# Two blocks of tokens held in two banks: 512-wide units for values, gates and queries of a four-layer network, and the sinks as a column of the scores

## The chip, the core and the metric

The program runs on one core of one Trainium2 chip. Its time is the device time of one execution in microseconds. The core has a matrix engine (PE, with its weight loads counted apart as PEld), three engines for vectors (DVE, ACT and POOL) and a queue (SP) that starts the loads of weights from HBM. All arithmetic that matters here is fp32: each product of matrices is made of three matrix multiplications of a high and a low part (high·high, high·low, low·high).

## The reference, cut to what matters

Four layers work on 512 tokens of width 1024. Layers 0 and 1 are attention layers with a gated FFN, layers 2 and 3 have an MLP with a squared ReLU. The change touches layers 1, 2 and 3:

```python
# layer 1 (NSA): q, the first 768 columns of the projection, and the 256 of the memory's queries
# layer 2 (gated linear attention), 4 heads of 256 value features each
q, k, v, g, glr = jnp.split(h @ w_in, [GLA_DK, 2 * GLA_DK, 2 * GLA_DK + GLA_DV, 2 * GLA_DK + 2 * GLA_DV], axis=-1)
log_a = jax.nn.log_sigmoid(glr @ w_gate_up + b_gate_up) / GLA_GATE_NORMALIZER
...
o = rms_norm(o, g_norm).reshape(B, T, GLA_DV)
o = o * jax.nn.silu(g.astype(jnp.float32))
return o.astype(h.dtype) @ w_out
# layer 3 (sliding window with sinks), per head
mx = jnp.maximum(jnp.max(s, axis=-1, keepdims=True), sink)
e = jnp.exp(s - mx)
p = e / (jnp.sum(e, axis=-1, keepdims=True) + jnp.exp(sink - mx))
```

## The kernel before

Tokens stand in four blocks of 128. A **weight unit** (`wunit`, L181) is 128x1024 numbers, 512 KB: SP loads it into `raw` (3 buffers), ACT copies it to the high part `whi` (L188), and DVE (in 2 pieces of 512) or POOL (in 4 of 256) makes the low part `wlo` (L175). `whi` and `wlo` have a few buffers each, so that a unit can be made ready while another is used. Matmuls stand on lines L198 to L200 (`mm3`, one line for each of the three products).

Where the result is wanted with tokens on the partitions, `tm_steps` takes a matrix of 1024x256 as two units, holds both, and goes through the four blocks one after the other. A block is 24 matmuls of 256 columns into a PSUM bank of its own, and then its evacuation. In layer 1, `q_steps` does this for the four groups 0, 3, 1, 2 of the queries with the tag "any", which takes banks from the tags `ps` and `tr` in turn (2 banks each, 4 together). In layer 2, `v_steps(h)` (values of head h) and `g_steps(h)` (its gates) do it with the tag `gm`, which has 2 banks. Those two banks also take the 512-wide query and key matrices of the next head (`unit`, called `gla_qk` unit below).

The evacuation of a block in layer 2: values are scaled on ACT (L1424) and their low part is made on DVE (L1425). Gates go through Silu on ACT (L1475), and POOL multiplies the norm's gain in (L1476). Silu, Exp, Ln and the square root (L243) use different function tables on ACT; a change of table is an instruction of its own, ACT_TABLE_LOAD.

Layer 2 is written as lists of steps that `weave` (L97) mixes: the log gates (`gate`: matmul, Abs L1459, Exp L1460; `gate_log`: Ln L1466) with `v_steps(1)`, then for each head h the steps of its linear attention (`gla_steps`: transposes, at, ke, qs, products into `more` and `acc`, Squares L1609) with a fill: for h = 0 the next head's query and key units, `g_steps(0)` and `g_steps(1)`, for h = 1 the units, `v_steps(2)` and `g_steps(2)`, for h = 2 the units and `v_steps(3)`, for h = 3 `g_steps(3)`. A scheduler then orders the instructions of each engine; each engine works its list strictly in order.

In layer 3 a task (`swa_task`) is a block of queries for two heads: scores on PE, mask and maximum on DVE (L1724), two Exp with a sum on ACT (L1726), then the sink: POOL adds the maximum to it (L1728), ACT takes its Exp (L1729), POOL adds that to the sum (L1732), and DVE takes the reciprocal (L1734); DVE and POOL normalize one head each (L436, L445), PE transposes.

Of the kernel before, what the change touches and what calls it, by code (L numbers as in the profile page):

```python
# [10 lines left out]
F32 = mybir.dt.float32  # L11
# [98 lines left out]
class Core:  # L110
# [33 lines left out]
    def t4(self, shape=(P, S), dt=F32):  # L144
        return self.sm(shape, "sm_s", 6, dt)
# [188 lines left out]
    def tm_steps(self, act, src, width, evac, tags=("gm",) * 4, eng=None, b0=0):  # L334

        box = {}

        def load():
            box["w"] = self.tm_weights(src, width, eng)

        def block(b):
            o = self.psum(tags[b])
            for k in range(KC):
                t = slice(b * P, (b + 1) * P)
                self.mm3(o[:, :width], self.part(act[k], t), box["w"][k], k == 0, k == KC - 1)
            evac(b, o)

        return [load] + [lambda b=b: block(b) for b in range(b0, NB)]

# [835 lines left out]
    def layer1(self):  # L1185
# [35 lines left out]
        def q_steps(g):  # L1221
            def first():
                tqs[g] = self.blk([P, NB, 256], F32, "tq")

            evac = lambda b, ps: self.evac_to(tqs[g], 256, rstd)(b, ps)
            return [first] + self.tm_steps(act, self.a["w_nsa"][g], 256, evac, ("any",) * 4)
# [11 lines left out]
        def prep(g):  # L1238
# [10 lines left out]
            if g == 3:  # L1249
# [7 lines left out]
        main = (kv_steps(0) + kv_steps(1) + [gates] + q_steps(0) + q_steps(3) + self.mem_steps(1, mkv) + q_steps(1)  # L1257
                + q_steps(2))
# [136 lines left out]
    def layer2(self):  # L1395
# [35 lines left out]
        def v_steps(h):  # L1431
            return self.tm_steps(act, self.a["w_gla"][h], 256, v_evac(h), eng=self.G)

# [37 lines left out]
        def g_steps(h):  # L1471
# [6 lines left out]
            return self.tm_steps(act, self.a["w_gla"][4 + h], 256, evac, eng=self.G)  # L1478

        gates = [functools.partial(f, b) for f in (gate, gate_log) for b in range(NB)]  # L1480
        weave(gates, (v_steps(1), 0, 1))
# [11 lines left out]
        for h in range(4):  # L1493
            fill, nxt = [], {}
            if h < 3:
                fill = [lambda h=h: nxt.update(self.gla_decay(h + 1, la, rb))]
                ps = []

                def unit(i, h=h):
                    o = self.gm()  # L1500
                    self.gemm_fm(act, [self.wunit(self.a["w_glaqk"][h + 1 + i], eng=self.G)], [o])
                    ps.append(o)

                fill += [lambda: unit(0), lambda: unit(4), lambda: self.gla_qk(nxt, *ps)]
                fill += g_steps(0) + g_steps(1) if h == 0 else (finals if h == 1 else []) + v_steps(h + 1) + (g_steps(2) if h == 1 else [])
            else:
                fill = g_steps(3)
# [119 lines left out]
    def layer3(self):  # L1627
# [48 lines left out]
        for u in range(2):  # L1676
            t, f = self.t2(), self.t2()
            self.V.tensor_tensor(t, outs[u], rb, ALU.mult)
            self.V.tensor_scalar(f, t, bias(u), None, ALU.add)
            if u == 0:  # L1680
                for g in range(2):
                    r, ro = slice(g * 64, g * 64 + 64), slice(64 - g * 64, 128 - g * 64)
                    self.A.activation(kh[g][r, 0], f[r], AF.Copy)
                    self.A.activation(kh[g][ro, 0], f[r], AF.Copy)
                    self.lo(kh[g][r, 1], f[r], kh[g][r, 0])
                    self.V.tensor_copy(kh[g][ro, 1], kh[g][r, 1].bitcast(F32))
            else:
                pt = self.gm()
# [16 lines left out]
    def swa_task(self, j, b, qT, kh, vv, bufs, ns):  # L1705
# [10 lines left out]
        def softmax():  # L1716
# [3 lines left out]
            w["p"] = p = self.t4()  # L1720
            for e in range(2):
                h = 2 * j + e
                o = slice(e * 256, e * 256 + n)
                self.V.tensor_tensor_reduce(p[:, o], sc[:, o], self.swa[:, 256 - n:256], -SCALE, ns[:, h:h + 1],  # L1724
                                            ALU.add, ALU.min, accum_out=m[:, e:e + 1])
                self.A.activation(p[:, o], p[:, o], AF.Exp, bias=m[:, e:e + 1], scale=-1.0, accum_out=z[:, e:e + 1])  # L1726
            w["sk"] = sk = self.lt([P, 2], "sk", 4)
            self.G.tensor_tensor(sk, self.sinks[:, 2 * j:2 * j + 2], m, ALU.add)  # L1728
            self.A.activation(sk, sk, AF.Exp)  # L1729

        def norm():
            self.G.tensor_tensor(w["z"], w["z"], w["sk"], ALU.add)  # L1732
            r = self.sm([P, 2], "nm_r", 6)
            self.V.reciprocal(r, w["z"])  # L1734
            for e in range(2):
                self.normalize(w["p"][:, e * 256:e * 256 + n], r[:, e:e + 1], None, "VG"[e])

        def trans():
            w["tr"] = tr = self.psum("tr")
            for e in range(2):  # L1740
                for c in range(n // P):
                    s = slice(e * 256 + c * P, e * 256 + (c + 1) * P)
                    self.T.transpose(tr[:, s], w["p"][:, s], self.ident)
# [75 lines left out]
def pack(i):  # L1819
# [32 lines left out]
    o["w_nsa"] = _tm(np.concatenate([nsa[:, 0:768], nsa[:, 1572:1828]], 1), 256)  # L1852
# [11 lines left out]
    o["w_gla"] = _tm(gla[:, 1024:3072], 256)  # L1864
# [29 lines left out]
```

## Time and profile before

| | us |
|---|---|
| median of 3 runs | 2370.29 (2369.07 to 2371.36) |
| the profiled execution's own time | 2370.64 |
| its span in the profile | 2368.9 |
| PE busy | 2321.1 |
| DVE busy | 1436.7 |
| ACT busy | 1131.7 |
| POOL busy | 482.0 |

The span is what the profile's views are measured in, from the first instruction to the last; the own time holds what lies around it, 1.7 us. PE is busy for 98% of the span, so most things that the other engines do lie beside it. Layer 1's projections stand at about 592 to 720 us, layer 2's gates, values and linear attention at 1284 to 1445, layer 3's attention at 1892 to 1980.

### The profile page before, as it was taken

The page shows a single profiled execution, that of the slowest core. Times are in us where ns is not written, and L with a number is a line of the kernel's source. Part 1 is how long each engine was busy: PE and PEld are TensorE (multiplying, and loading weights), DVE is VectorE, ACT ScalarE, POOL GpSimd, SP SyncE. Part 2 cuts the span into 40 slices and gives each one's busy share as a digit, 9 for nine tenths or more (in the row PEclk, how much of TensorE's full clock was granted, in tenths as well). Part 3 has the DMA queues.
Part 4 walks back from the last instruction along what each step waited for, and adds up shares of the span by engine and source line. Part 5 has one row for each costly group of instructions (what it writes and reads, how often), then busy time and mean ns, then how long its engine had stood idle before and what let it go on. Part 6 is the DMA issues. An engine that isn't in the chain of part 4 may idle for free.

```text
span 2368.9 us, 35404 instructions
## 1 busy us (share of the span) xinstructions
PE 2321.1 (98%) x13390; PEld 2004.4 (85%) x13390; DVE 1436.7 (61%) x2980; ACT 1131.7 (48%) x2152; POOL 482.0 (20%) x738
## 2 busy tenths in 40 slices
PE   8899999999999999999999999999999999999998
PEld 8888988888997879888888998988888878988886
DVE  5996655455667676554555446744446787644446
ACT  7677522222458675222226566633225686533233
POOL 2756000000137730000001660000000171000000
PEclk9999999999999999999999999999999999999999
DMA  5213422322330114223222224432224414423224
GB/s 179 72 37 101 149 100 90 99 97 98 101 132 21 63 46 142 99 90 101 95 94 77 81 68 155 160 101 97 96 98 160 143 55 130 163 86 104 97 100 142
DMA packets 68301, 243.88 MB, mean 103 GB/s; under 512 B 7570, under 2 KB 7826, under 8 KB 68131
## 3 DMA queue, kind: packets, MB, share of 16 engines
q1 hardware_dynamic: 68130, 241.62, 30.9%
q8 instruction: 106, 1.74, 0.3%
q14 instruction: 65, 0.52, 0.1%
HBM read 239.50 MB, written 2.10 MB: 102 GB/s over the span
## 4 chain that ended last, share of the span: by engine, by line
PE 89%; DVE 7%; ACT 3%; issue 1%; DMA 1%; POOL 0%; SPq 0%; DVEq 0%; ACTq 0%; POOLq 0%
PE ps L199 11%; PE ps L200 11%; PE ps L198 11%; PE tr L198 11%; PE tr L199 11%; PE tr L200 10%; PE gm L199 3%; PE gm L198 3%; PE gm L200 3%; PE acc L529 2%; PE more L198 2%; PE more L199 2%; PE more L200 2%; PE tr L451 2%; PE ps L424 1%; PE ps L425 1%
## 5 line engine op out<-in xcount | busy, mean ns | idle before, releaser
L188 ACT ACTIVATE whi<-raw 128x1024 fp32r<-128x1024 f32 (+1 forms) x443 | 466.2, 1054 | 857.2 <-PE ps L199 223.3
L175 DVE TENSOR_TENSOR wlo<-raw,whi 128x512 fp32r<-128x512 f32 x744 | 525.7, 749 | 318.4 <-ACT whi L188 316.9
L175 POOL TENSOR_TENSOR wlo<-raw,whi 128x256 fp32r<-128x256 f32 x284 | 220.0, 805 | 628.6 <-ACT whi L188 540.6
L199 PE MATMUL ps<-act,whi 128*128 128x512 f32 (+1 forms) x712 | 257.3, 362 | 0.1
L198 PE MATMUL ps<-act,whi 128*128 128x512 f32 (+1 forms) x712 | 257.3, 362 | 0.1
L200 PE MATMUL ps<-act,wlo 128*128 128x512 f32 (+1 forms) x712 | 257.1, 361 | 0.1
L200 PE MATMUL tr<-act,wlo 128*128 128x512 f32 (+1 forms) x640 | 231.6, 362 | 0.0
L198 PE MATMUL tr<-act,whi 128*128 128x512 f32 (+1 forms) x640 | 231.5, 362 | 0.0
L199 PE MATMUL tr<-act,whi 128*128 128x512 f32 (+1 forms) x640 | 231.3, 361 | 0.0
L731 POOL TENSOR_TENSOR sm_s<-sm_s,sm_s 128x512 f32<-128x512 f32 x40 | 51.7, 1292 | 531.9 <-DVE sm_s L730 531.9
L198 PEld LDWEIGHTS ps<-act,whi 128*128 128x128 f32 x712 | 134.3, 189 | 20.7 <-ACT whi L188 0.3
L199 PEld LDWEIGHTS ps<-act,whi 128*128 128x128 f32 x712 | 134.3, 189 | 20.7 <-DVE act L302 0.3
L200 PEld LDWEIGHTS ps<-act,wlo 128*128 128x128 f32 x712 | 134.3, 189 | 20.5 <-DVE wlo L175 0.2
L199 PEld LDWEIGHTS tr<-act,whi 128*128 128x128 f32 x640 | 120.8, 189 | 18.4
L200 PEld LDWEIGHTS tr<-act,wlo 128*128 128x128 f32 x640 | 120.9, 189 | 18.4
L198 PEld LDWEIGHTS tr<-act,whi 128*128 128x128 f32 x640 | 120.8, 189 | 18.3
L445 POOL TENSOR_TENSOR sm_s<-sm_s,nm_r 128x256 f32<-128x256 f32 (+2 forms) x172 | 105.1, 627 | 45.7 <-DVE nm_r L479 23.5
L178 ACT ACTIVATE hid<-sm_s 128x512 fp32r<-128x512 f32 x88 | 55.6, 632 | 109.7 <-DVE sm_s L884 58.1
L198 PE MATMUL gm<-whi,act 128*128 128x256 f32 (+1 forms) x360 | 102.9, 288 | 1.3 <-ACT rb L280 0.6
L200 PE MATMUL gm<-whi,act 128*128 128x256 f32 (+1 forms) x360 | 102.2, 286 | 0.0
L199 PE MATMUL gm<-wlo,act 128*128 128x256 f32 (+1 forms) x360 | 101.8, 285 | 0.0
L199 PE MATMUL ps<-wlo,hid 128*128 128x512 f32 x256 | 99.8, 390 | 0.0
(665 smaller groups left out, 5810.0 us busy)
## 6 DMA issues: line engine op xcount, KB each, us to landing
raw<-in_w_down SPq DMA_DIRECT2D x124, 512.0 KB, 3.3
raw<-in_w_ffn SPq DMA_DIRECT2D x96, 512.0 KB, 3.3
raw<-in_w_up SPq DMA_DIRECT2D x80, 512.0 KB, 3.4
raw<-in_w_o SPq DMA_DIRECT2D x32, 512.0 KB, 3.3
raw<-in_w_glao SPq DMA_DIRECT2D x16, 512.0 KB, 3.4
raw<-in_w_swa SPq DMA_DIRECT2D x16, 512.0 KB, 3.4
raw<-in_w_swao SPq DMA_DIRECT2D x16, 512.0 KB, 3.3
raw<-in_w_dsa SPq DMA_DIRECT2D x14, 512.0 KB, 3.7
```

Source lines behind the costliest of these rows:

```text
L175: (eng or self.V).tensor_tensor(out, src, hi.bitcast(F32), ALU.subtract)
L178: self.A.activation(hi, src, AF.Copy)
L188: self.A.activation(hi[:, :n], raw[:, :n], AF.Copy)
L198: mm(out, l[0], r[0], start=start, stop=False)
L199: mm(out, l[0], r[1], start=False, stop=False)
L200: mm(out, l[1], r[0], start=False, stop=stop)
L424: self.T.matmul(out, q[:, t], k[0][:, k0:k0 + n], start=True, stop=False)
L425: self.T.matmul(out, q[:, t], k[1][:, k0:k0 + n], start=False, stop=True)
L445: self.G.tensor_tensor(p, p, r.to_broadcast([P, p.shape[-1]]), ALU.mult)
L451: self.T.transpose(ps[:, s], p[:, s], self.ident)
L529: return self.T.matmul(acc[e * 64:e * 64 + 64, t0:t0 + p[e].shape[-1]], v[e], p[e], start=start and i == 0, stop=stop and i == n - 1)
L731: self.G.tensor_tensor(u, u, t, ALU.mult)
```

## The change

A new function `tm_wide` takes a matrix of 1024x512 as four units; a unit is two of the eight chunks of 128 input features, 512 columns wide. It holds two blocks' results at once in two banks. Pass 0 goes through the units 0, 1, 2, 3 for blocks 0 and 1 and then evacuates both, pass 1 goes backwards through 3, 2, 1 for blocks 2 and 3 and ends with unit 0, which is loaded and split a second time. So a matrix takes five units where two matrices of 256 took four. Layer 1's queries become two such matrices. In layer 2 the values of head i+1 and the gates of head i become one for i = 0, 1, 2 (`vg_steps`), with the low part on DVE where it was on POOL; the last head's gates stay 256 wide. The fills change with it: the gates of layer 2 are woven with `vg_steps(0)`, h = 0 with the units and `vg_steps(1)`, h = 1 with the units and `vg_steps(2)`, h = 2 with the units alone, h = 3 with the last gates. In layer 3 the sink becomes a column of the scores' tile, which POOL copies in ahead; the Exp takes one column more and its sum holds the sink.

```diff
+    def tm_wide(self, act, src, evac, tag="gm", eng=None):
+        units, box = {}, {}
+        def step(p, i):
+            if i not in units:
+                units[i] = self.wunit(src[:, i * 1024:(i + 1) * 1024], eng=eng)
+            a, z = ((0, 3), (3, 0))[p]
+            if i == a:
+                box["ps"] = [self.psum(tag) for _ in range(2)]
+            self.tok_unit(units[i], act[2 * i:2 * i + 2], box["ps"], (2 * p, 2 * p + 1), i == a, i == z)
+            if i == z:
+                for b, o in zip((2 * p, 2 * p + 1), box["ps"]):
+                    evac(b, o)
+            if i == 0:
+                units.pop(0)
+        return [functools.partial(step, 0, i) for i in range(4)] + [functools.partial(step, 1, i) for i in (3, 2, 1, 0)]
...
-        main = (kv_steps(0) + kv_steps(1) + [gates] + q_steps(0) + q_steps(3) + self.mem_steps(1, mkv) + q_steps(1)
-                + q_steps(2))
+        main = (kv_steps(0) + kv_steps(1) + [gates] + q_steps(0, (0, 3)) + self.mem_steps(1, mkv)
+                + q_steps(1, (1, 2)))
...
+        def vg_steps(i):
+            box = {}
+            def first():
+                box["e"] = v_evac(i + 1), g_evac(i)
+            def evac(b, ps):
+                for n, e in enumerate(box["e"]):
+                    e(b, ps[:, n * 256:n * 256 + 256])
+            return [first] + self.tm_wide(act, self.a["w_glvg"][i], evac)
...
-        weave(gates, (v_steps(1), 0, 1))
+        weave(gates, (vg_steps(0), 0, 1))
...
-                fill += g_steps(0) + g_steps(1) if h == 0 else (finals if h == 1 else []) + v_steps(h + 1) + (g_steps(2) if h == 1 else [])
+                fill += (finals if h == 1 else []) + (vg_steps(h + 1) if h < 2 else [])
...
-            w["p"] = p = self.t4()
+            w["p"] = p = self.t4(S + 2).rearrange("p (e k) -> p e k", e=2)
+            self.G.tensor_copy(p[:, :, n], ns[:, 2 * j:2 * j + 2])
...
-                self.A.activation(p[:, o], p[:, o], AF.Exp, bias=m[:, e:e + 1], scale=-1.0, accum_out=z[:, e:e + 1])
-            w["sk"] = sk = self.lt([P, 2], "sk", 4)
-            self.G.tensor_tensor(sk, self.sinks[:, 2 * j:2 * j + 2], m, ALU.add)
-            self.A.activation(sk, sk, AF.Exp)
+                self.A.activation(p[:, e, :n + 1], p[:, e, :n + 1], AF.Exp, bias=m[:, e:e + 1], scale=-1.0,
+                                  accum_out=z[:, e:e + 1])
...
-            self.G.tensor_tensor(w["z"], w["z"], w["sk"], ALU.add)
```

In layer 3 the bias of the keys and values is also added by ACT as it copies, where DVE added it before.

The order of the instructions, first in the kernel before. On PE, at the end of the gates of head 1, the third block's bank (gm_13494) ends and the fourth block (gm_13521) begins:

```order
L200 MATMUL gm_13494<-whi_13406,act_12624 128x256
L198 MATMUL gm_13494<-whi_13406,act_12625 128x256
L199 MATMUL gm_13494<-wlo_13407,act_12625 128x256
L200 MATMUL gm_13494<-whi_13406,act_12625 128x256
L198 MATMUL gm_13521<-whi_13397,act_12618 128x256 [waits Activation_49]
L199 MATMUL gm_13521<-wlo_13398,act_12618 128x256
L200 MATMUL gm_13521<-whi_13397,act_12618 128x256
```

And on ACT, the evacuations of the four banks of the same gates (sg), with what stands between them:

```order
L1475 ACTIVATE sg_13118<-gm_13432,r_2428_12726 128x256 [waits PE_49]
L1475 ACTIVATE sg_13118<-gm_13459,r_2428_12726 128x256 [waits PE_49]
L1609 ACTIVATE t_2538_13492,oss_13122<-acc_13414 128x256 [waits PE_49]
L243 ACT_TABLE_LOAD
L243 ACTIVATE rs_s_13557<-mv_13555 128x4 [waits DVE_49]
L1475 ACT_TABLE_LOAD
L1475 ACTIVATE sg_13118<-gm_13494,r_2428_12726 128x256 [waits PE_49]
L188 ACTIVATE whi_13651<-raw_13650 128x1024 [waits DMAHW5_49,PE_49,Pool_49]
L1475 ACTIVATE sg_13118<-gm_13521,r_2428_12726 128x256 [waits PE_49]
```

Here 24 matmuls of a block stand between the end of a bank and the next use of that bank, as gm has two.

The first place in the changed kernel, on PE: the end of the first wide matrix of layer 2 (banks gm_12868 and gm_12869, values of head 1 and gates of head 0, blocks 2 and 3), and behind it the first query unit of the next head (gm_13001):

```order
L198 MATMUL gm_12869<-whi_12911,act_12433 128x512
L199 MATMUL gm_12868<-wlo_12912,act_12433 128x512 [waits DVE_49]
L200 MATMUL gm_12868<-whi_12911,act_12433 128x512
L199 MATMUL gm_12869<-wlo_12912,act_12433 128x512
L200 MATMUL gm_12869<-whi_12911,act_12433 128x512
L1602 MATMUL tr_12961<-qd_12946,sm_s_12945 128x64 [waits DVE_49]
L198 MATMUL gm_13001<-act_12432,whi_13003 128x512 [waits Activation_49]
```

And on ACT, where these two banks are evacuated (values L1448, gates L1496):

```order
L188 ACTIVATE whi_13037<-raw_13036 128x1024 [waits DMAHW4_49,PE_49]
L1448 ACTIVATE v_12761<-gm_12868,r_2426_12540 128x256 [waits PE_49]
L1448 ACTIVATE v_12761<-gm_12869,r_2426_12540 128x256 [waits PE_49]
L188 ACTIVATE whi_13095<-raw_13094 128x1024 [waits DMAHW5_49,DVE_49,Activation_49]
L1496 ACT_TABLE_LOAD
L1496 ACTIVATE sg_12762<-gm_12868,r_2426_12540 128x256 [waits DVE_49]
L1496 ACTIVATE sg_12762<-gm_12869,r_2426_12540 128x256 [waits DVE_49]
```

The query unit takes the bank of gm_12868, and three matmuls stand between that bank's last matmul and it; the gates' evacuation, which frees the bank, stands behind two evacuations of values, a copy of a weight unit and a change of table.

The second place, the end of the second wide matrix (gm_13215 and gm_13216), on PE, with the query unit of head 2 (gm_13338) behind it; L1602 and L1603 are small products of the linear attention:

```order
L200 MATMUL gm_13215<-whi_13262,act_12433 128x512
L198 MATMUL gm_13216<-whi_13262,act_12433 128x512
L199 MATMUL gm_13216<-wlo_13263,act_12433 128x512
L200 MATMUL gm_13216<-whi_13262,act_12433 128x512
L1602 MATMUL ps_13372<-qd_12984,sm_s_12983 128x64
L1603 MATMUL ps_13372<-qd_12984,sm_s_12982 128x64
L1602 MATMUL ps_13372<-qd_12984,sm_s_12983 128x64
L1603 MATMUL ps_13372<-qd_12984,sm_s_12982 128x64
L1602 MATMUL ps_13372<-qd_12984,sm_s_12983 128x64
L1603 MATMUL ps_13372<-qd_12984,sm_s_12982 128x64
L198 MATMUL gm_13338<-act_12432,whi_13340 128x512 [waits Activation_49]
```

And on ACT there (cat is the copy of head 0's gated output out of PSUM):

```order
L1448 ACTIVATE v_13077<-gm_13215,r_2426_12540 128x256 [waits PE_49]
L178 ACTIVATE cat_13302<-tr_13304 128x512
L178 ACTIVATE cat_13303<-ps_13305 128x512
L1448 ACTIVATE v_13077<-gm_13216,r_2426_12540 128x256 [waits PE_49]
L188 ACTIVATE whi_13497<-raw_13496 128x1024 [waits DMAHW4_49,DVE_49,Activation_49]
L1496 ACT_TABLE_LOAD
L1496 ACTIVATE sg_13078<-gm_13215,r_2426_12540 128x256 [waits DVE_49]
L1605 ACTIVATE t_2572_13381<-ps_13372 128x512 [waits PE_49]
```

Nine matmuls stand on PE between the last one of gm_13215 and the reuse of its bank; six instructions of ACT stand between the moment at which that bank is full and the end of its evacuation, and the evacuation itself makes seven.

The third place, the change from pass 0 to pass 1 of the second wide matrix, on ACT (t is a Square of the linear attention's output, fd a copy of its state):

```order
L1448 ACTIVATE v_13076<-gm_13101,r_2426_12540 128x256 [waits PE_49]
L1646 ACTIVATE t_2531_13149,oss_12960<-more_13079 128x256 [waits PE_49]
L1448 ACTIVATE v_13076<-gm_13102,r_2426_12540 128x256 [waits PE_49]
L1646 ACTIVATE t_2542_13213,oss_12960<-acc_13197 128x256 [waits DVE_49,PE_49]
L178 ACTIVATE fd_13210<-t_2540_13208 128x256 [waits DVE_49]
L1496 ACTIVATE sg_13078<-gm_13101,r_2426_12540 128x256 [waits DVE_49]
L1496 ACTIVATE sg_13078<-gm_13102,r_2426_12540 128x256 [waits DVE_49]
```

On PE two 512-wide and nine 256-wide matmuls stand between the last one of gm_13101 and the first of pass 1, which takes the same bank.

## Rows read from the trace of the kernel before

**Rows 1.** The page: busy time by engine, and the chain that ended last by engine.

```profile
PE 2321.1 (98%) x13390; PEld 2004.4 (85%) x13390; DVE 1436.7 (61%) x2980; ACT 1131.7 (48%) x2152; POOL 482.0 (20%) x738
...
PE 89%; DVE 7%; ACT 3%; issue 1%; DMA 1%; POOL 0%; SPq 0%; DVEq 0%; ACTq 0%; POOLq 0%
```

**Rows 2.** Windows, layer 1's projections, layer 2, layer 3's attention: stretch, length, busy times, clock.

```profile
592.00:720.00 128.00, 127.02 (x967) 121.85 (x967) 76.20 (x144) 65.23 (x126) 33.68 (x45) 1.00 0.33 109
1284.00:1445.00 161.00, 159.63 (x1132) 148.46 (x1132) 78.72 (x152) 96.24 (x168) 84.51 (x107) 0.99 0.23 76
1892.00:1980.00 88.00, 84.09 (x539) 66.99 (x538) 73.92 (x252) 71.93 (x228) 54.05 (x128) 1.00 0.24 78
```

**Rows 3.** Waits of PE, 1284 to 1445: total us, times, longest us.

```profile
PE gm L198 <- ACT rb L280: 0.6, 1, 0.6
```

**Rows 4.** Timeline of PE in layer 2: start, duration, instruction, count.

```profile
1301.80 0.28 PE L198 MATMUL gm<-whi,act 128*128 128x256 f32 x1
1301.92 0.28 PE L199 MATMUL gm<-wlo,act 128*128 128x256 f32 x1
...
1302.16 1.50 PE L1529 MATMUL ps<-consts,la 128*128 128x128 f32 x12
...
1304.43 0.39 PE L199 MATMUL gm<-act,whi 128*128 128x512 f32 x1
...
1306.95 0.39 PE L198 MATMUL gm<-act,whi 128*128 128x512 f32 x1
```

**Rows 5.** Groups of ACT, 1284 to 1445: busy, mean ns, idle before.

```profile
L188 ACT ACTIVATE whi<-raw 128x1024 fp32r<-128x1024 f32 x24 | 25.3, 1056 | 18.9 <-PE gm L199 7.2 <-issue 6.1 <-PE gm L200 3.4
L1475 ACT ACTIVATE sg<-gm,r 128x256 f32<-128x256 f32 x16 | 7.5, 474 | 10.4 <-PE gm L200 10.3
L1475 ACT ACT_TABLE_LOAD x5 | 6.4, 1283 | 0.1
...
L1424 ACT ACTIVATE v<-gm,r 128x256 fp32r<-128x256 f32 x12 | 5.6, 467 | 5.3 <-PE gm L200 5.3
...
L178 ACT ACTIVATE fd<-t 128x256 fp32r<-128x256 f32 x12 | 4.9, 417 | 2.3 <-DVE t L1602 1.5 <-DVE t L1604 0.7
...
L1609 ACT ACTIVATE t<-acc 128x256 f32<-128x256 f32 x8 | 3.0, 379 | 2.6 <-PE acc L200 2.5
...
L178 ACT ACTIVATE cat<-tr 128x512 fp32r<-128x512 f32 x3 | 1.8, 589 | 0.0
...
L1609 ACT ACTIVATION_READ_ACCUMULATOR t<-acc 128x1 f32 x8 | 1.6, 196 | 0.0
...
L1568 ACT ACTIVATE t<-ps 128x512 f32<-128x512 f32 x2 | 1.2, 603 | 0.8 <-PE ps L1566 0.8
```

**Rows 6.** Timeline of ACT at the log gates of layer 2.

```profile
1294.66 0.60 ACT L1459 ACTIVATE ge<-tr 128x512 f32<-128x512 f32 x1
1295.29 0.63 ACT L1460 ACTIVATE ge<-ge 128x512 f32<-128x512 f32 x1
1295.94 1.28 ACT L1466 ACT_TABLE_LOAD   x1
1297.24 0.72 ACT L1466 ACTIVATE ge<-ge,ones 128x512 f32<-128x512 f32 x1
```

**Rows 7.** Windows ahead of a fall of the clock and behind it, and around a gap without one.

```profile
72.00:76.80 4.80, 1.90 (x17) 1.72 (x17) 4.63 (x10) 3.44 (x13) 3.90 (x5) 1.00 0.52 168
76.80:80.40 3.60, 3.60 (x20) 3.60 (x20) 3.42 (x12) 1.28 (x4) 0.47 (x1) 0.53 0.01 3
...
148.50:158.90 10.40, 9.94 (x54) 8.29 (x51) 9.08 (x41) 8.14 (x32) 3.84 (x8) 0.51 0.07 29
...
835.50:838.50 3.00, 0.96 (x5) 0.54 (x5) 1.24 (x7) 2.80 (x6) 0.40 (x3) 1.00 0.00 0
838.50:842.00 3.50, 3.25 (x21) 1.96 (x22) 3.12 (x10) 2.67 (x8) 0.82 (x1) 1.00 0.00 0
```

**Rows 8.** Groups of layer 3's sinks, 1892 to 1980.

```profile
L1729 ACT ACTIVATE sk<-sk 128x2 f32<-128x2 f32 x32 | 5.6, 192 | 0.6 <-POOL sk L1728 0.6
```

More of the change, by code (lines that the diff above doesn't have):

```diff
@@ L142, in t2, with t4 @@
         return self.sm(shape, "t2", 3, dt)
-    def t4(self, shape=(P, S), dt=F32):
-        return self.sm(shape, "sm_s", 6, dt)
+    def t4(self, n=S):
+        return self.sm([P, S + 2], "sm_s", 6)[:, :n]
     def fd(self, shape=(P, S), dt=F32):
@@ L1219, in layer1, with q_steps @@
         tqs, qT, cTs = [None] * 4, [None] * KC, [None] * 3
-        def q_steps(g):
+        def q_steps(i, gs):
             def first():
-                tqs[g] = self.blk([P, NB, 256], F32, "tq")
-            evac = lambda b, ps: self.evac_to(tqs[g], 256, rstd)(b, ps)
-            return [first] + self.tm_steps(act, self.a["w_nsa"][g], 256, evac, ("any",) * 4)
+                for g in gs:
+                    tqs[g] = self.blk([P, NB, 256], F32, "tq")
+            def evac(b, ps):
+                for n, g in enumerate(gs):
+                    self.evac_to(tqs[g], 256, rstd, n * 256)(b, ps)
+            return [first] + self.tm_wide(act, self.a["w_nsa"][i], evac, "any")
         kT, vT = [], []
@@ L1469, in layer2, with g_evac @@
         sgs = {}
-        def g_steps(h):
+        def g_evac(h):
             sgs[h] = sg = self.blk([P, NB, 256], F32, "sg")
@@ L1504, in layer2 @@
                 fill += [lambda: unit(0), lambda: unit(4), lambda: self.gla_qk(nxt, *ps)]
-                fill += g_steps(0) + g_steps(1) if h == 0 else (finals if h == 1 else []) + v_steps(h + 1) + (g_steps(2) if h == 1 else [])
+                fill += (finals if h == 1 else []) + (vg_steps(h + 1) if h < 2 else [])
             else:
-                fill = g_steps(3)
+                fill = g_steps()
             weave(prev + self.gla_steps(cur, vp.pop(h)), (fill, 0, 1))
@@ L1676, in layer3 @@
         for u in range(2):
-            t, f = self.t2(), self.t2()
+            t = self.t2()
             self.V.tensor_tensor(t, outs[u], rb, ALU.mult)
-            self.V.tensor_scalar(f, t, bias(u), None, ALU.add)
             if u == 0:
@@ L1682, in layer3 @@
                     r, ro = slice(g * 64, g * 64 + 64), slice(64 - g * 64, 128 - g * 64)
[L1683 to L1686, printed above, removed]
-            else:
+                    bs = bias(u)[r]
+                    for i in (r, ro):
+                        self.A.activation(kh[g][i, 0], t[r], AF.Identity, bias=bs)
+                        self.V.scalar_tensor_tensor(kh[g][i, 1], t[r], bs, kh[g][r, 0].bitcast(F32), ALU.add, ALU.subtract)
+            else:
+                f = self.t2()
+                self.A.activation(f, t, AF.Identity, bias=bias(u))
                 pt = self.gm()
@@ L1735, in norm @@
             for e in range(2):
-                self.normalize(w["p"][:, e * 256:e * 256 + n], r[:, e:e + 1], None, "VG"[e])
+                self.normalize(w["p"][:, e, :n], r[:, e:e + 1], None, "VG"[e])
         def trans():
@@ L1742, in trans @@
                     s = slice(e * 256 + c * P, e * 256 + (c + 1) * P)
[L1743 removed]
+                    self.T.transpose(tr[:, s], w["p"][:, e, c * P:(c + 1) * P], self.ident)
         def s2():
@@ L1863, in pack @@
     o["w_down"] = np.stack([_down(f("ffn_w_down")[l]) for l in range(2)])
-    o["w_gla"] = _tm(gla[:, 1024:3072], 256)
+    gv, gg = gla[:, 1024:2048], gla[:, 2048:3072]
+    o["w_glvg"] = np.stack([_tm(np.concatenate([gv[:, h * 256 + 256:h * 256 + 512], gg[:, h * 256:h * 256 + 256]], 1), 512)[0]
+                            for h in range(3)])
+    o["w_glg"] = _tm(gg[:, 768:1024], 256)[0]
     o["w_glv"] = _tm(np.concatenate([gla[:, 1024:1280], gla[:, 3072:3088]], 1), 272)[0]
```

14 lines of the change are left out of this document (7 added, 7 removed).

## The prediction

> **What bounds the kernel now.** I read the page first. PE is busy for 2321.1 of 2368.9 us and holds 89% of the chain that ended last [rows 1], so a step on another engine counts only where PE has to wait for it. The windows of the three stretches that are touched say how near PE is to its limit in each [rows 2]: in layer 1's projections it idles 1.0 us of 128, in layer 2 1.4 of 161, in layer 3's attention 3.9 of 88. The longest wait of PE in layer 2 is 0.6 us, and it stands before the gates [rows 3]: the evacuations there, which end in ACT's Silu, are all hidden at present. That hiding is what I look at below, since ACT has only 96.24 of the 161 us filled and would look idle enough from the page.
>
> **What the wide matmuls save.** The durations mislead: 0.28 us for 256 columns and 0.39 for 512, but neighbours overlap. The starts tell the cost [rows 4]: 0.12 us from one 256-wide matmul to the next, and (1306.95 - 1304.43)/11 = 0.229 us for the 512-wide, 11 of which start in that time. Two narrow ones cost 0.240, one wide 0.229: 0.011 us saved. A matrix of 1024x512 has 3 x 8 x 4 = 96 wide matmuls, so a pair of old matrices saves 1.06 us. Layer 1 has two such pairs, -2.1 us, layer 2 three, -3.2 us. Together -5.3, which needs a PE without waits.
>
> **What the reload costs.** Each pair loads and splits a fifth unit: one more `whi` copy of 1.056 us on ACT [rows 5]. Five of them stand beside PE, since ACT has over 60 us free in each of the stretches of layers 1 and 2 [rows 2]. Unit 0's second copy takes the buffer of unit 3, the first one that pass 1 is done with, and has two units, 24 matmuls or 5.5 us, before it is wanted. I take nothing. If its cover were gone, PE would wait for copy and low part once in each pair; the copy alone is 5.3 us in all.
>
> **Banks in layer 1.** The tag "any" has four banks; the second pass takes the other two, so an evacuation has 48 matmuls or 11 us of cover. Nothing.
>
> **Banks in layer 2.** Here `gm` has two, both are full at the same time at the end of a pass, and the next user of `gm` waits until the first of them is empty. That bank is emptied by two ACT evacuations (values 0.467, gates 0.474 us) with DVE's part between, and ACT takes them in its own order, with other work and a change of table (1.283 us) in between [rows 5]. Before, one block lay between the end of a bank and its next use, 24 x 0.12 = 2.9 us. Each place is PE's work up to the reuse of the bank against ACT's up to the end of its evacuation; small matmuls count 1.50/12 = 0.125 us [rows 4].
> - End of matrix 1 (first place of the order): ACT has values twice, a weight copy, a table, the gates: 0.934 + 1.056 + 1.283 + 0.474 = 3.75 us. PE has two wide ones and a small one, 0.58. Stall 3.2.
> - End of matrix 2 (second place): values twice 0.934, `cat` twice 1.178, weight copy 1.056, table 1.283, gates 0.474: 4.93. PE: three wide, six small, 1.44. Stall 3.5.
> - End of matrix 3: as the last, with one copy of 0.603 more (t from ps), 5.53. PE: three wide and ten small, 1.94. Stall 3.6.
> - Pass change in matrix 2 (third place): two values 0.934, two Squares with their reads 2 x 0.575, fd 0.417, gates 0.474: 2.97. PE: 2 x 0.229 + 9 x 0.12 = 1.54. Stall 1.4.
> - Pass change in matrix 3: only the second Square's result is late: behind the first Square's matmuls stand 1.2 us of PE against 0.575 + 0.575 + 0.474 on ACT. Stall 0.4.
> - Pass change in matrix 1, among the log gates: from the last gate's matmul ACT has Abs, Exp and a table, 1297.24 - 1294.66 = 2.58, four Ln of 0.72 [rows 6], values 0.467, a table, gates 0.474: 7.7. PE has 23 wide and 8 small, 6.3. Stall 1.4.
> - The last head: its gates lost the fill around them; behind `qs` stand a table and Silu, 1.76, against 8 narrow matmuls, 0.96. Stall 0.8.
>
> Sum 14.3 us. In each of these waits everything of PE stands still, the linear attention's products among it; ACT, DVE and POOL get no later than PE. So the stall is not made up: PE was full before. If the gates' evacuations came ahead of the table and the weight copy, the sum would fall to near 0; if DVE's part of the values is late too (its row before is hidden), it grows. I keep 5 to 18 as ends.
>
> **Does a change of table cost more than its row?** The row of the load says 1.28 us, and its neighbours stand close: Exp ends at 1295.92, the load goes from 1295.94 to 1297.22, Ln begins at 1297.24 [rows 6]. So 1.28 is the whole price here and the sum goes by that. The Trainium skill, "ScalarE: Activation LUTs", section "What ACT_TABLE_LOAD costs", gives about 1283 ns for the load and about 1380 ns of drain with it, some 2.66 us for every switch. The trace agrees on the load and shows no drain. What a dearer switch would do is the third rival.
>
> **The clock.** After 2.9 us without work in the 4.8 us to 76.8, PE's granted clock fell to about half (0.53) for 3.6 us; another fall lasted 10.4 us (0.51). A gap of 2.0 us in a stretch of 3.0 was followed by no fall [rows 7]. A fall of 3.6 us loses 3.6 x 0.47 = 1.7 us of work, one of 10.4 loses 5.1. Three of the stalls above (3.2, 3.5, 3.6) are longer than 2.9. I count falls of the short kind behind two of them, +3.4; the ends are 0 and 3 x 5.1 = 15.
>
> **Layer 3.** ACT loses 32 small Exp, 32 x 0.192 = 6.1 us, of a stretch in which it is busy 71.93 of 88 and DVE 73.92 [rows 2, 8]. POOL loses two small additions a task and gains one copy, which stands in POOL's list behind its normalizations, and DVE's mask waits for it. The copy has no row; it is bounded by nothing (hidden, as POOL has 34 us free) and by the 6.1 us that ACT gives back. PE idles 3.9 us there: between 0 and 6.1 I take half of the idle time, -2. The bias on ACT instead of DVE is a few instructions ahead of the attention: nothing.
>
> **Sum.** -5.3 + 14.3 - 2 + 3.4 = +10.4. Own time 2370.64 + 10.4 = 2381.0; the median of the runs is 0.35 below the profiled execution, so 2380.7 us. A change under 0.2% (4.7 us) can't be told from none here.
>
> **The rivals.**
> - Faster: the Silu of a pass's first bank runs as soon as the bank is full, so PE waits no more than before. Then -5.3 and layer 3's -2 to -6 stay: 2361 (2359 to 2363). For it: ACT idles 65 us of layer 2's 161. Against: ACT's list is worked in order, and it has a table and a weight copy ahead of the gates at the end of each of the three matrices. It decides if the stalls of all seven places together are below some 2.6 us. Chance 0.14.
> - No change: half of the hand sum, 7.2, against -5.3 and -2, no fall of the clock: 2370 (2366 to 2375). For it: I let ACT begin each chain only when the bank is full, and have PE's rows at their shortest. Chance 0.2.
> - Slower by more: a switch of table holds ACT for another 1.28 us at five of the places (the three ends, the first pass change, the last head): +6.4, 2387. That is the drain that the page names. The rows above speak against it. Or each of the three long stalls brings a fall of the clock of the long kind, up to 2392. Chance of both 0.1.
> - My forecast, 2380.7 (2375 to 2386): chance 0.56.
>
> **How the numbers follow.** The range goes from the upper part of the faster case, 2364, to the long falls, 2390; that leaves out most of the faster case (0.11) and the tail above (0.06). Of the forecast's own 0.56 all lies above the bound of 2375.0; with the dearer cases slower has 0.66, no change 0.2, faster 0.14.
>
> **What would show it.** Right: in layer 2, PE waits for ACT's gates (sg) at the bank of the first matmul of the three query units or output products behind each wide matrix, 3 us and more each, and 14 us in all; layer 1's projections shorter by about 2 us; no ACT Exp of the sinks and an attention of 86 us. Wrong: no PE wait over 1 us between 1284 and 1445, which would bring the faster case; or a wait of DVE for POOL's copy in layer 3 that pulls PE with it, which would add to the time where I take some off.

## The result

| | us |
|---|---|
| before, median of 4 runs | 2369.76 (2369.07 to 2371.36) |
| changed, median of 4 runs | 2392.1 (2390.11 to 2393.1) |
| ratio | 1.0083, interval 1.0071 to 1.0096 |

By the medians the change makes the kernel slower by 22.3 us, by the ratio by 0.83%, 19.7 us; the interval holds both. That is the way that was forecast, but about twice the size (+10.4). The median lies 2 us above the upper end of the range, 2390, and 2369.76 times the ratio, 2389.4, just below it. In the profiled executions the span went from 2368.9 to 2390.6 us.

### Where it went, by stage

Two instructions that stand in both kernels mark the stages: the transposes at the start of layer 2's log gates (L1446 before, L1467 after) and those of layer 3's values (L1690, L1728). First the kernel before, by source line (count, duration ns as least/median/most, first and last start):

```profile
L1446 PE MATMUL tr<-consts,gl x4: 272/272/273, 1283.5 to 1283.8; 128*16 128x128 f32 x4
...
L1690 PE MATMUL gm<-consts,t x4: 270/272/272, 1885.3 to 1885.6; 128*128 128x128 f32 x4
```

The same in the changed kernel:

```profile
L1467 PE MATMUL tr<-consts,gl x4: 272/272/273, 1289.1 to 1289.5; 128*16 128x128 f32 x4
...
L1728 PE MATMUL gm<-consts,t x4: 270/272/272, 1908.6 to 1908.9; 128*128 128x128 f32 x4
```

Up to the log gates the changed kernel is 5.6 us late, up to layer 3's values 23.3, at the end 21.7. So layers 0 and 1 lost 5.6, layer 2 with its MLP 17.7, and layer 3 with its MLP gave 1.6 back. Layer 0 is the same code in both, and 0.6 of the 5.6 lie ahead of layer 1: its first 274-wide matmul starts at 617.56 before and at 618.15 after. That leaves 5.0 for layer 1. My terms for layers 1, 2 and 3 were -2.1, +14.5 (-3.2 + 14.3 + 3.4) and -2.

### The profile after

The page, busy time by engine; PE has 4.7 us more of it than in [rows 1] with fewer instructions, as matmuls at half clock count for longer:

```profile
PE 2325.8 (97%) x12910; PEld 1986.0 (83%) x12910; DVE 1449.4 (61%) x3012; ACT 1135.2 (47%) x2127; POOL 440.6 (18%) x658
```

The waits of PE in the changed kernel's layer 2, 1284 to 1470 (total us, times, longest):

```profile
PE gm L198 <- ACT sg L1496: 10.1, 4, 4.3
PE tr L1659 <- DVE sg L1657: 2.1, 1, 2.1
PE tr L1618 <- DVE t L1614: 0.9, 1, 0.9
PE acc L198 <- ACT t L1646: 0.7, 1, 0.7
PE gm L198 <- ACT rb L280: 0.6, 1, 0.6
PE more L198 <- ACT at L178: 0.5, 1, 0.5
```

The first row is the predicted wait: a matmul into `gm` waits for the gates' Silu that still reads the bank. All rows together are 14.9 us; before, the same stretch had 1.3, the longest 0.6 [rows 3]. The four waits of the first row are 0.64 at the pass change of matrix 1, and 3.56, 4.30 and 1.56 at the ends of the three matrices. The timeline of PE at the end of the first wide matrix (start, duration, and at a row's end the idle time and what ended it):

```profile
1318.91 0.39 PE L199 MATMUL gm<-wlo,act 128*128 128x512 f32 x1
1319.14 0.39 PE L200 MATMUL gm<-whi,act 128*128 128x512 f32 x1
1319.37 0.33 PE L1602 MATMUL tr<-qd,sm_s 128*128 128x64 f32 x2
1323.26 0.50 PE L198 MATMUL gm<-act,whi 128*128 128x512 f32 x1 [3.56 <-ACT sg L1496]
```

and of ACT at the same time:

```profile
1319.11 0.93 ACT L1448 ACTIVATE v<-gm,r 128x256 fp32r<-128x256 f32 x2 [1.21 <-PE gm L200]
1320.36 1.06 ACT L188 ACTIVATE whi<-raw 128x1024 fp32r<-128x1024 f32 x1 [0.32 <-DMA raw<-in_w_glvg]
1321.43 1.28 ACT L1496 ACT_TABLE_LOAD   x1
1322.73 0.84 ACT L1496 ACTIVATE sg<-gm,r 128x256 f32<-128x256 f32 x2
```

Values, weight copy, change of table, gates: the chain is link by link the one of the prediction's first place. The stall is 3.56 us where 3.2 were worked out; 0.32 of it is a wait of the weight copy for its load, which I had not counted. The load of the table takes 1.28 us, and 0.02 after it Silu starts, so the drain of the Trainium skill, "ScalarE: Activation LUTs", section "What ACT_TABLE_LOAD costs", does not show here either, and the rival that rests on it falls.

Layer 1 is where I expected nothing but a gain. The waits of PE there, 680 to 760 us:

```profile
PE ps L444 <- ACT sm_s L652: 7.2, 3, 5.6
PE gm L198 <- DVE t L598: 1.7, 1, 1.7
PE gm L1387 <- DVE cs L1382: 0.5, 1, 0.5
PE acc L549 <- DVE qT L175: 0.4, 1, 0.4
PE tr L471 <- DVE pt L539: 0.2, 1, 0.2
```

Before, the same stretch held 5.5 us of waits, none over 1.3. The 5.6 us stand at the scores of the memory's attention, and the view names ACT's Exp. But ACT itself was idle then; the timeline of DVE tells who was late (L648 and L649 make the maximum that the Exp needs, L435 to L438 are the rope of the queries):

```profile
720.56 0.69 DVE L648 TENSOR_REDUCE mm_m<-ps 128x2 f32<-128x512 f32 x1 [4.23 <-PE ps L445]
721.28 0.24 DVE L649 TENSOR_SCALAR mm_m<-mm_m 128x2 f32<-128x2 f32 x1
721.44 1.03 DVE L435 TENSOR_TENSOR t<-tq,consts 128x256 f32<-128x256 f32 x1
722.39 1.37 DVE L436 TENSOR_TENSOR t<-tq,consts 128x128 f32<-128x128 f32 x1
...
726.00 0.80 DVE L437 TENSOR_TENSOR t<-tq,consts 128x128 f32<-128x128 f32 x1
726.73 0.41 DVE L438 TENSOR_TENSOR tq<-t,t 128x256 f32<-128x256 f32 x1
727.06 0.68 DVE L648 TENSOR_REDUCE mm_m<-ps 128x2 f32<-128x512 f32 x1
```

Seven instructions of the rope of two groups stand between the first maximum and the second (the cut leaves out three of them). Before, the queries of groups 1 and 2 were ready one after the other, and only the last instruction of one rope (L418) stands between the first two maxima.

The third loss is the clock. Windows over the stretches in layers 1 and 2 in which the granted clock had fallen (the column behind POOL's):

```profile
1325.00:1328.20 3.20, 3.20 (x9) 2.43 (x9) 0.00 (x0) 0.00 (x0) 0.03 (x1) 0.50 0.63 241
1372.60:1376.00 3.40, 3.39 (x8) 2.71 (x9) 1.52 (x2) 2.05 (x4) 3.37 (x4) 0.50 0.54 153
1440.90:1451.00 10.10, 9.51 (x42) 8.68 (x43) 5.34 (x11) 5.46 (x10) 1.34 (x2) 0.50 0.01 2
686.50:689.90 3.40, 3.27 (x15) 3.27 (x16) 3.31 (x7) 2.72 (x5) 2.56 (x4) 0.50 0.38 139
727.50:734.20 6.70, 4.34 (x20) 4.05 (x21) 5.72 (x19) 4.07 (x16) 5.02 (x9) 0.50 0.25 78
```

In layer 2 these are 16.7 us at half clock, 8.4 us of work lost if PE had work all the time; before there was one fall of 3.4 us, 1.7 lost, and it came with no wait of PE over 0.6 us in the 8 us ahead of it. The first of the three begins 1.5 us after the end of the wait of 3.56 us, the second right at the end of the wait of 4.30, the long one in PE's wait of 2.1 us for DVE's gating. In layer 1 there are 10.1 us against 3.4 before. Layer 2's MLP ends with a fall in both kernels, this one before and one of 3.4 us at 1901.6 after:

```profile
1875.70:1882.60 6.90, 6.15 (x15) 4.83 (x16) 5.04 (x9) 2.90 (x5) 3.34 (x5) 0.51 0.50 169
```

With that the stages can be added up. Layer 1: -2.1 for the pitch, +4.5 of waits (10.0 against 5.5), +3.4 of clock: 5.8, and 5.0 were found. Layer 2 with its MLP: -3.2 for the pitch, +13.6 of waits (14.9 against 1.3), +5.0 of clock (+6.7 for the three falls, -1.7 for the shorter one at the end): 15.4, and 17.7 were found. The difference lies where the pitch's saving should be. If the length of this stage is freed of PE's idle time and of half of its time at half clock, about 593 us are left before, and in the seven traces with wide matrices in layer 2 only 0.3 to 2.0 us less, 1.2 in the changed kernel, not the 3.2 (or 2.1 for two matrices) that the rows of the pitch give. What takes the rest is not shown.

### The profile page after: what moved, and what is told of

Read it like the earlier page. It is cut to its first block, busy times and chain, and to the rows that moved or that the text cites. A ratio compares the mean times of both kernels' runs of the same rounds, so it can differ in the third digit from the quotient of the medians.

```text
span 2390.6 us, 34399 instructions
## 1 busy us (share of the span) xinstructions
PE 2325.8 (97%) x12910; PEld 1986.0 (83%) x12910; DVE 1449.4 (61%) x3012; ACT 1135.2 (47%) x2127; POOL 440.6 (18%) x658
## 5 line engine op out<-in xcount | busy, mean ns | idle before, releaser
L188 ACT ACTIVATE whi<-raw 128x1024 fp32r<-128x1024 f32 x448 | 471.6, 1055 | 876.3 <-PE ps L199 219.0
L175 DVE TENSOR_TENSOR wlo<-raw,whi 128x512 fp32r<-128x512 f32 (+1 forms) x778 | 549.2, 748 | 342.2 <-ACT whi L188 340.6
L175 POOL TENSOR_TENSOR wlo<-raw,whi 128x256 fp32r<-128x256 f32 x236 | 183.3, 808 | 202.3 <-ACT whi L188 194.6
L200 PE MATMUL ps<-whi,hid 128*128 128x512 f32 x256 | 99.7, 389 | 0.0
L198 PE MATMUL ps<-whi,hid 128*128 128x512 f32 x256 | 99.6, 390 | 0.0
L450 ACT ACTIVATE sm_s<-sm_s,sm_m 128x128 f32<-128x128 f32 (+3 forms) x144 | 80.6, 570 | 18.4 <-DVE sm_m L449 18.2
```

The source lines that it names most:

```text
L175: (eng or self.V).tensor_tensor(out, src, hi.bitcast(F32), ALU.subtract)
L188: self.A.activation(hi[:, :n], raw[:, :n], AF.Copy)
L198: mm(out, l[0], r[0], start=start, stop=False)
L200: mm(out, l[1], r[0], start=False, stop=stop)
L450: self.A.activation(p, p, AF.Exp, bias=m, scale=-1.0, accum_out=z)
```

## The experiments

All are given as the ratio to the kernel before, run beside them on the same chip, with the 95% interval; the medians of before lay between 2372.3 and 2373.1 us there, so 0.1% is 2.4 us. A trace is one execution out of 5 to 11 of its kernel.

### The three parts alone

Each kernel is the one before with the hunks of one layer of the change.

**Layer 1 alone.**

> The kernel before with the wide queries of layer 1 alone. The traces of before and after put about +5 us on layer 1. Theory A (layer 1's own order on DVE: the maxima of the memory's attention stand behind the rope of the queries, PE waits about 6 us once, and the clock falls for longer): before plus 4 to 6 us, 2374 to 2376. Rival (the +5 us in layer 1 are an effect of the changes elsewhere, the wide queries themselves save the 2 us that the pitch gives): before minus 2 us, about 2368.

Measured 1.0011 (1.0002 to 1.0020), 2374.92 us against 2372.70, +2.2: less than theory A says, and not the rival's gain.

**Layer 2 alone.**

> The kernel before with the wide values and gates of layer 2 alone. Theory A (PE waits for the gates' evacuation at the reuse of the two gm banks, some 15 us, and the clock falls behind the long waits, some 7 us, against 3 us saved): before plus 17 to 20 us, 2387 to 2390. Rival (layers 1 and 2 disturb each other, or layer 3's order is the cause): clearly less than plus 17.

Measured 1.0067 (1.0054 to 1.0080), 2388.58 us, +15.9. In its trace the waits for the gates are 9.9 us, as in the whole change, but the clock is at half no longer than before: one fall of 3.4 us at 1366.2 in the linear attention, and 6.8 us at the MLP's end. The stage is 13.5 us longer all the same, 14.1 of it waits. So the waits are the cause that stays, and the 5 us of clock are not in every execution.

**Layer 3 alone.**

> The kernel before with the sinks as a column in layer 3 (and the bias on ACT) alone. Theory A (32 small Exp less on ACT and 32 POOL additions less, in a stretch in which ACT and DVE are nearly full): before minus 2 to 3 us, 2367. Rival (POOL's copy in its queue holds DVE's mask up, the saving is lost): before, 2369 to 2371.

Measured 0.9993 (0.9984 to 1.0001), 2370.15 us, -2.5 by the medians; the interval reaches 1, so these runs alone do not show a gain. The traces speak for one: from layer 3's values (L1690) to the end, the four kernels with this part take 482.0 to 482.5 us, the ten without it 483.5 to 485.5.

The three come to 0.71% together against 0.83% (0.71 to 0.96) of the whole: layer 2 holds most of it by itself, and no large part comes from one layer disturbing another. Layer 1 lost less by these runs than in the profile. Its traces do not bear that out: from the first 274-wide matmul to the log gates, the four kernels with both wide matrices take 670.3 to 672.7 us, the eight that leave layer 1 as it was 665.7 to 668.4. The interval of the runs reaches up to 4.7 us, and which is nearer stays open.

### Layer 2: the bank or the fill?

**DVE empties the gates' half of the bank**, in the whole change:

```diff
-                self.A.activation(sg[:, b], ps[:, :256], AF.Silu, scale=r12[:, b:b + 1])
+                V.tensor_scalar(sg[:, b], ps[:, :256], r12[:, b:b + 1], None, ALU.mult)
+                self.A.activation(sg[:, b], sg[:, b], AF.Silu)
```

> The changed kernel with one edit: the gates' half of a bank is scaled out of PSUM by DVE, and Silu then works in SBUF, so that no change of table stands between a full bank and its release. Theory A (the waits at the gm banks are waits for ACT's table and Silu): the waits of PE on the gates' evacuation fall from 10 us in the view of waits to a few us, the clock falls in layer 2 become fewer, and the time goes from 2392 to about 2377 (2373 to 2382). Rival B (the reload and the low parts on DVE make the units late, DVE is the bound of layer 2): 16 more instructions of 0.48 us on DVE make it no better, 2391 to 2396.

Measured 1.0046 (1.0033 to 1.0059), 2385.01 us. The wait for the gates went from 10.1 to 0.9 us as expected, but the time fell by 9 us (by the ratios) and not by 15. Rival B falls, as it is better with more work on DVE; theory A alone doesn't do either. Other waits had grown, those for DVE's gating from 2.1 to 5.7 us, and they point to the fill: the change also moved work from head 2 to the log gates. **Layer 2 alone with the same edit** shows it:

> Layer 2's wide matrices alone, placed as in the change, with the gates' half of a bank scaled out of PSUM by DVE. Together with layer 2 alone (plus 15.9 us), the fill of before with Silu on the bank (plus 2.2) and the fill of before with DVE's copy (0) it fills the table of two by two. Theory A alone (banks): before plus 0 to 3 us. Theory A with D (banks and moved fill, each for itself): before plus 5 to 8. The whole kernel with this edit lay at plus 12.3, with layer 1's and 3's parts in it.

Measured 1.0036 (1.0022 to 1.0051), 2379.97 us, +7.2. Its waits of PE in layer 2:

```profile
PE tr L1656 <- DVE sg L1654: 5.7, 3, 2.4
PE gm L198 <- DVE sg L1492: 0.9, 1, 0.9
PE acc L198 <- ACT t L1643: 0.7, 1, 0.7
```

That is what theories A and D together gave. In the first row PE waits for DVE to gate a head's output, 2.35, 1.19 and 2.13 us at the ends of heads 0, 1 and 2. At head 2 the head's chain (Square, square root, reciprocal, gating) is there as before, and the matmuls of the next values no longer lie beside it. The waits at heads 0 and 1 are not in the changed kernel's trace; they come up where PE is no longer held at the banks. **The fill moved with nothing made wide** tests that by itself:

```diff
-        weave(gates, (v_steps(1), 0, 1))
+        weave(gates, (v_steps(1) + g_steps(0), 0, 1))
...
-                fill += g_steps(0) + g_steps(1) if h == 0 else (finals if h == 1 else []) + v_steps(h + 1) + (g_steps(2) if h == 1 else [])
+                fill += (finals if h == 1 else []) + (v_steps(h + 2) + g_steps(h + 1) if h < 2 else [])
```

> The kernel before with all matrices 256 wide, one load per unit and one evacuation per block, but with the fill of layer 2 placed as the change places it: values of head 1 and gates of head 0 among the log gates, values 2 and gates 1 at head 0, values 3 and gates 2 at head 1, nothing at head 2. Theory D (heads 2 and 3 lack PE work beside their chain): before plus 4 to 7 us, with waits of PE on DVE's gating at the ends of heads. Theory A (the two banks filled at once are nearly the whole loss): before to before plus 2 us.

Measured 1.0030 (1.0019 to 1.0041), 2379.64 us, +6.9, as theory D says. The wait is there, without a wide matmul in the layer:

```profile
PE tr L1622 <- DVE sg L1620: 3.9, 2, 3.6
```

The wait of 3.6 us stands at the end of head 2. A fall of the clock of 10.1 us follows it, and the fall among the log gates, 3.4 us before, is 10.2 us long here:

```profile
1430.70:1440.80 10.10, 9.64 (x44) 8.78 (x44) 4.44 (x9) 5.70 (x11) 2.33 (x3) 0.50 0.01 2
1294.10:1304.30 10.20, 10.20 (x42) 8.47 (x41) 5.25 (x9) 8.33 (x15) 0.00 (x0) 0.50 0.00 0
```

In this trace layer 2 with its MLP is 8.1 us longer than before, 3.1 of it waits and 5.1 clock. The two are not separated by a run, and layer 2 alone with DVE's copy had one fall of 3.4 us in its linear attention and lost as much by its runs.

**Wide matrices with the fill left where it was.** Two wide ones: gates 0 with gates 1 at head 0, values 2 with gates 2 at head 1; values 1, values 3 and gates 3 stay 256 wide.

```diff
-        weave(gates, (vg_steps(0), 0, 1))
+        weave(gates, (one_steps(0), 0, 1))
...
-                fill += (finals if h == 1 else []) + (vg_steps(h + 1) if h < 2 else [])
+                fill += (finals if h == 1 else []) + (two_steps(h) if h < 2 else one_steps(1))
```

> The kernel before with two wide matrices in layer 2, placed so that each head keeps the fill that it had before: the values of head 1 stay 256 wide among the log gates, the gates of heads 0 and 1 are one wide matrix at head 0, the values and gates of head 2 one at head 1, the values of head 3 stay 256 wide at head 2, the last gates as before. Silu reads the bank, as in the changed kernel. Theory A (the banks' release behind Silu and the table is the main loss): before plus 8 to 12 us, as two of the three long waits stay. Theory D (the loss is mainly that heads 2 and 3 lost the matmuls that stood beside their chain, DVE's gating and ACT's copies): before plus 0 to 4.

Measured 1.0009 (1.0000 to 1.0018), 2374.52 us, +2.2: theory D's range. The gates hold PE for 2.3 us here, in two waits. And with DVE's copy as above:

> The same two wide matrices in layer 2 with the fill of before, and in addition the gates' half of a bank is scaled out of PSUM by DVE with Silu in SBUF. If theories A and D together hold the whole loss of layer 2, no long wait is left and the pitch's saving shows: before minus 2 us (minus 4 to plus 1). If the reload or the low parts on DVE cost something of their own, it stays 4 us or more above before.

Measured 0.9999 (0.9990 to 1.0008), 2372.90 us against 2372.31. The longest waits in layer 2, with DVE's copy, 0.65 of the first row at head 0, 1.19 at head 1 and none at head 2:

```profile
PE tr L1656 <- DVE sg L1654: 1.8, 2, 1.2
PE gm L198 <- ACT rb L280: 0.6, 1, 0.6
```

Together:

| | 256 wide | wide, Silu reads the bank | wide, DVE empties the bank |
|---|---|---|---|
| fill as before | 1 | 1.0009 | 0.9999 |
| fill as changed | 1.0030 | 1.0067 | 1.0036 |

Read down a column, the moved fill costs 0.30% with nothing wide, 0.58 where Silu reads the bank and 0.37 where DVE empties it. Read along a row, the bank's release behind Silu costs 0.31 (0.67 less 0.36) with the moved fill, and 0.10 with the fill as before, which is within the intervals of the two runs. So the moved fill costs by itself, and the two cost more together than each alone. The upper row has two wide matrices and the lower three, so what the third, among the log gates, adds is not separated. The saving of the pitch, 2.1 us or 0.09% for two matrices, is not to be told from none in the last column: it may be eaten by the gating's waits that are left, 1.8 us, or lie in the interval.

### Layer 1: one of the two matrices

**Rope of group 2 on POOL**, with both matrices wide:

```diff
-                self.rope(tqs[g].rearrange("p b (h d) -> p b h d", d=64), 4, self.V)
+                self.rope(tqs[g].rearrange("p b (h d) -> p b h d", d=64), 4, self.G if g == 2 else self.V)
```

> Layer 1's wide queries alone, with the rope of group 2 on POOL in place of DVE. Theory A (the maximum of the memory's attention stands behind two ropes on DVE, as both groups come at once): three instructions of 0.8 us leave DVE ahead of the maximum, the longest wait of PE there falls from 5.6 to about 3 us, and the time is 2 to 3 us less than layer 1's wide queries alone, about that of before. Rival (the waits there come from ACT's evacuations of the wide banks): the wait stays at 5 to 6 us.

Measured 1.0018 (1.0009 to 1.0027), 2377.51 us, +5.2 by the medians. The wait:

```profile
PE ps L444 <- ACT sm_s L652: 6.7, 4, 4.3
PE ps L444 <- DVE sm_m L449: 1.8, 3, 0.7
```

The longest fell from 5.6 to 4.3, others came, and the time did not fall; the profiled execution, 2373.25 us, was the fastest of its eleven. So the two ropes are what DVE did during the wait, but taking one off DVE doesn't bring the time back.

**The first matrix alone** (groups 0 and 3 wide, 1 and 2 as before):

> Layer 1 with the first wide matrix (groups 0 and 3) alone; groups 1 and 2 stay 256 wide, one after the other. Theory A: the wait of 5.6 us goes, as the ropes come apart again; what is left is the wait of 1.7 us for the memory's keys and a fall of the clock there, against 1 us saved: before to before plus 2 us. Rival (the first matrix is the cause, as it shifts all that follows): before plus 4 or more.

Measured 1.0029 (1.0021 to 1.0038), 2379.04 us, +6.7, the most of all. **The second alone** (groups 1 and 2 wide, 0 and 3 as before):

> Layer 1 with the second wide matrix (groups 1 and 2) alone, ahead of the memory's attention; groups 0 and 3 stay 256 wide. In the run with both the long wait stood behind two ropes in a row on DVE, in the run with the first matrix alone the layer lost more than with both. Theory A (two ropes come at once and stand ahead of the memory's maximum): before plus 2 to 5 us with a wait of 3 to 6 us at the first scores of the memory's attention. Theory E (the order in which the memory's keys and the first matrix share PE, DVE and the clock is what costs, the second matrix costs nothing): before minus 1 to plus 1.

Measured 1.0002 (0.9993 to 1.0011), 2372.78 us against 2372.74: theory E's range. The second matrix costs nothing by itself, and the first, without two ropes at once, costs the most, so theory A is not the whole. This run doesn't refute it: in its trace three instructions of the first rope stand ahead of the first maximum, and four more between the first two maxima, where with both matrices wide all seven stood. The waits, first of the kernel with the first matrix wide, then of that with the second:

```profile
PE ps L444 <- ACT sm_s L652: 3.4, 2, 2.4
PE gm L198 <- ACT whi L188: 2.1, 1, 2.1
PE tr L471 <- ACT pt L537: 2.1, 1, 2.1
PE tr L199 <- DVE wlo L175: 1.1, 1, 1.1
```

```profile
PE gm L198 <- DVE t L598: 2.4, 1, 2.4
PE ps L444 <- ACT sm_s L652: 2.2, 3, 1.4
PE tr L471 <- ACT pt L537: 2.1, 1, 2.1
```

With the first matrix wide, a weight unit comes 2.1 us late at the memory's keys and a low part 1.1 us late, and the memory's scores wait again. The unit is late because its load is: ACT waits for the memory's key units,

```profile
ACT whi L188 <- DMA raw<-in_w_memk: 7.7, 2, 5.1
```

and the second of them is issued at 681.49, lands at 685.25, and ACT copies it at 685.27. Before, ACT waited for none of them; with the second matrix wide it waited 6.7 us for them, and the time didn't change. So what costs lies in the first matrix and the stretch behind it, where its units, the memory's and the keys' DVE work meet. Which of these waits is the cause, and why both matrices together cost less than the first alone, stays open.

### The parts that cost nothing, put together

Two wide matrices in layer 2 with the fill of before and DVE's copy, the sinks as a column in layer 3, layer 1 as before:

> The parts that cost nothing or saved time, together: two wide matrices in layer 2 with the fill of before and DVE's copy out of the banks (ratio 0.9999), and the sinks as a column in layer 3 (ratio 0.9993); layer 1 as before. If the parts add up: before minus 1 to 3 us, ratio 0.9988 to 0.9996, clearly faster than the changed kernel (about 20 us) and hardly to be told from before. If DVE, which has more to do now, carries a delay into layer 3: before or above.

Measured 0.9985 (0.9976 to 0.9994), 2368.96 us against 2373.06: faster than both kernels, by 4.1 us against the one before, a little more than the parts add up to, though that is under the 0.2% set as the bound at the outset.

## Why the prediction was right, and where it was short

The direction and its mechanism were right: PE waits for the gates' evacuation where two banks are full at once. About half of the loss was missing from the sum. That the result came out near 2392, the time of the three long falls in the third rival, is luck: one long fall came, and not behind a bank.

- **What bounds the kernel**: right. PE was full, and PE's waits in layer 2, +13.6 us, came out as lost time.
- **The pitch**: the rows were read rightly (one wide for two narrow saves 0.011 us, not the 0.17 that the durations would give; in the rows after, wide matmuls start 0.23 us apart again). The term was too large even so: layer 2 gained 0.3 to 2.0 us where it says 3.2 (2.1 for two matrices). No run shows the saving by itself.
- **The reload**: in layer 2 the copy cost nothing that shows, but for 0.32 us of waiting for a load in the chain that frees the bank. In layer 1 loads came late around the memory's keys; what the reload has to do with it is not shown.
- **Banks in layer 2**: the mechanism was right, and at the ends of matrices 1 and 2 place by place (3.56 and 4.3 us found, 3.2 and 3.5 worked out). At the end of matrix 3 the wait was 1.56 for 3.6, as PE had more to do there and waited 0.9 for DVE first; of the three pass changes one showed (0.64 for 1.4), and the last head none. That the sum of all waits, 13.6, lies near 14.3 is luck: only 10.1 are waits for the gates, and the rest were not in the sum. I had noted that head 3's gates lost their fill, 0.8 us, and not that head 2 had none at all. The moved fill costs 0.30% with nothing wide, so near half of layer 2's loss.
- **The clock in layer 2**: mis-sized. +3.4 was taken for two short falls; three came, one of 10.1 us, +6.7 against before. In the trace of layer 2 alone none was added. The rows that I had picked, a gap of 2.9 us with a fall and one of 2.0 without, said too little: in the same trace a fall at 1292 had no gap ahead of it.
- **"Banks in layer 1 ... Nothing"**: the step that failed. It looked at banks and the reload alone, and took over the layer's -2.1. In the profile the layer lost 5.0 us, by itself 2.2 in the runs (0.11%). The change also sets when the queries of a group come to DVE and which units are loaded around the memory's keys, and DVE and ACT have long chains there.
- **Layer 3**: the size was right, -1.6 in the profile for -2, and -0.07% alone. The sign that I had named, a shorter attention, is not there: from the first mask to the last 61.9 us before and 63.2 after. PE's idle time from the values to the last product fell from 4.9 to 3.7 us.
- The rival "faster" had the evacuations hidden, and "no change" half of them; 10.1 us of 14.3 were not hidden. That a change of table costs more than its row is not seen: Silu starts 0.02 us after the load. The long falls of the clock, the other half of the third rival, came once.

## What to carry to other kernels

When matmuls are made wider, ask what each bank's release waits for at the moment at which all banks of the tag are full at the same time: behind weight copies and changes of table on ACT the waits came to 10.1 us, and an engine that only copies the result out took them to 0.9. Then ask which chain loses the work that lay beside it: the same change of fill cost 7 us with nothing made wide. And a gain of 1 us for each matrix is worth trying only where the order of everything else stays, so each layer's part is best tried alone: one of the three here seems to help, two cost time.

## What the runs showed of the hardware

The clock does not fall at the same places from one trace to the next, even where the code is the same. Layer 0 is not touched by the change; the windows over two stretches of it, in the kernel before:

```profile
61.90:65.20 3.30, 3.30 (x31) 3.30 (x30) 2.14 (x5) 1.18 (x3) 2.29 (x3) 1.00 0.51 159
109.70:116.40 6.70, 6.70 (x58) 6.70 (x59) 6.70 (x17) 4.76 (x18) 4.36 (x6) 1.00 0.24 82
```

and in the changed kernel:

```profile
61.90:65.20 3.30, 3.30 (x18) 3.30 (x17) 1.58 (x2) 0.57 (x2) 2.10 (x3) 0.50 0.56 159
109.70:116.40 6.70, 6.22 (x30) 6.22 (x31) 6.64 (x18) 4.98 (x18) 5.64 (x8) 0.50 0.37 127
148.50:158.90 10.40, 7.98 (x63) 6.04 (x63) 10.40 (x46) 9.15 (x35) 4.80 (x9) 1.00 0.30 99
```

In the second kernel PE runs at 1.2 GHz in the first two stretches, and at 2.4 in the third, where the kernel before had fallen [rows 7]. The other experiments leave layer 0 alone too: of the fourteen traces, six have a fall of 10.2 us that begins at 148 to 152 us, two have one of 3.4 at 152 to 155, and six have none there. One profile alone can therefore place a few us on a stage that other executions don't have there. In layer 0 little came of it: after 17.0 us at half clock against 13.6, the changed kernel is 0.6 us late at layer 1, as the waits there are shorter where PE is slower (PE is busy for 9.94 of the 10.40 us at half clock in [rows 7], and for 7.98 at full clock above).
